# Two matmuls with a GELU between: b's first load ahead of a's, two banks for the first transposes, a's first cast on two engines

## The chip, the core and the metric

The kernel runs on one core of a Trainium2 chip. The metric is the device time of one execution in microseconds (us), taken as the median of several executions.

## The reference

```python
def reference(a, b, c):                 # a 1024x1024, b 1024x2048, c 2048x1024, all float32
    h = np.matmul(a, b)
    h = 0.5 * h * (1 + np.tanh(np.sqrt(2 / np.pi) * (h + 0.044715 * h ** 3)))
    return np.matmul(h, c).astype(np.float32)
```

So two products with a tanh-approximated GELU between them.

## The kernel before

The matmuls run in bf16 (and, in the later stages, on fp32 sums made from bf16 pieces); everything accumulates in fp32 in PSUM, whose eight banks are named by number (`bank(i)`). The order of work on every engine is the order in which the Python code issues it: the kernel uses a manual schedule, and only waits are derived from the tiles. An instruction therefore stands in the queue of its engine behind everything written above it for that engine.

The work has three stages. The first (lines 214 to 294) computes the first 512 columns of h, transposed, in eight blocks of 128 x 512: `ps[h, t]` is tile t (0 to 3) of h's columns for row half h (0 or 1) of a. The second stage (`seven(zero, ...)` and `seven(one, ...)`) makes the other 1536 columns of h, the third (`seven(two, ...)`) the product with c; both use seven products of half-size blocks in place of eight, with sums and differences made on VectorE (DVE). The change touches the first stage only.

**Loads.** The first stage starts with nothing in SBUF. SyncE (SP) issues twelve loads of 512 KB each (lines 76 to 82): `load_a(h, q)` brings 256 columns (q of 4) of row half h of a, `load_b(q)` brings two 128-row tiles of b's first 512 columns. They arrive as fp32 in the staging tiles `sta` and `stb`. All loads of b's other columns and of c are issued by GpSimd (POOL) behind a copy (`gate`, line 84) that waits for a late load of a.

**From a load to a product.** A piece of b needs one cast to bf16: `cast_b(k)` (line 136) is one ScalarE (ACT) instruction into `b1`, or, with n=2, two on half the columns each. A piece of a needs more, since TensorE wants it transposed: `cast_a(h, q, *engs)` casts 128 x 1024 elements into a bf16 tile `ab`, on one engine or in two halves on the engines named (line 99 is ACT, line 101 DVE). `turn(h, q, i, ab)` is a generator: at each `next` it issues four TensorE transposes into one half of the PSUM tile `pt` (line 132) and one DVE copy of that half to `aT` (line 133). Its two steps bring the k tiles 2q and 2q+1. In the kernel before both steps write halves of the same bank.

**Products.** `block(h, tiles, ks)` issues for each k in ks and each t in tiles one matmul of 128 x 128 weights (from `b1`) by 128 x 512 (from `aT`), all on line 105. `stir(*widths)` (line 116) issues matmuls of a zeroed fp32 tile whose result nobody reads, to keep TensorE busy while it would wait; one call shows as two records for each width.

**The order around the change** (before, lines 214 to 238): four fillers of width 256; the cast of a's piece (0, 0) on DVE alone; its transposes in bank 4 with fillers between; b's tiles 0 and 1; the cast of a's piece (1, 0) on DVE and ACT; six products of row half 0; the transposes of (1, 0), in bank 7, around two more products; then the first products of row half 1 (line 234) into banks 4, 5 and 6. From there on, loads, casts, transposes and products alternate in the same way (lines 239 to 294).

Of the kernel before, what the change touches and what calls it, by code (L numbers as in the profile page):

```python
# [11 lines left out]
BF16 = mybir.dt.bfloat16  # L12
# [7 lines left out]
def kernel(ctx, tc, a, b, c, out):  # L20
    nc = tc.nc
    M, K = a.shape
    _, N = b.shape
    _, P = c.shape
    H = 512
# [17 lines left out]
    def bank(i, shape=(128, H), dt=F32, name="ps"):  # L43
        return pp.tile(list(shape), dt, name=name, tag=f"bank{i}", padded_shape=None)

    def pieces(tag, bufs, shape, dt, name):
        return small.tile(shape, dt, name=name, tag=tag, bufs=bufs)
# [21 lines left out]
    def load_a(h, q):  # L69
        nc.sync.dma_start(out=sta[q // 2][:, h, q % 2],  # L70
                          in_=av[:, 4 * h:4 * h + 4, ds(q * 256, 256)])

    def load_b(q):
        nc.sync.dma_start(out=stb[:, 2 * q:2 * q + 2], in_=bv[:, 2 * q:2 * q + 2, 0:H])

    load_a(0, 0)
    load_b(0)
    load_a(1, 0)
    for q in range(1, 4):
        load_a(0, q)  # L80
# [16 lines left out]
    def copy(eng, dst, src):  # L97
        if eng is nc.scalar:
            nc.scalar.activation(dst, src, AF.Copy)  # L99
        else:  # L100
            nc.vector.tensor_copy(dst, src)  # L101
# [11 lines left out]
    def stir(*widths):  # L113

        for w in widths:
            nc.tensor.matmul(ps[0, 3][:, 0:w], warm[:, 0:128], warm[:, 0:w],  # L116
                             start=True, stop=True, skip_group_check=True)

    def cast_a(h, q, *engs):

        ab = pieces("ab", 2, [128, 4, 256], BF16, "ab")
        for i, eng in enumerate(engs):
            w = 256 // len(engs)
            copy(eng, ab[:, :, ts(i, w)], sta[q // 2][:, h, q % 2][:, :, ts(i, w)])
        return ab

    def turn(h, q, i, ab):

        pt = bank(i, (128, 2, H), BF16, "pt")
        for n in range(2):  # L130
            for m in range(4):
                nc.tensor.transpose(pt[:, n, ts(m, 128)], ab[:, m, ts(n, 128)], ident)  # L132
            nc.vector.tensor_copy(aT[:, h, 2 * q + n], pt[:, n])  # L133
            yield

    def cast_b(k, n=1):
        for i in range(n):
            r = ds(i * (H // n), H // n)
            nc.scalar.activation(b1[:, k, r], stb[:, k, r], AF.Copy)  # L139

    def block(h, tiles, ks):
        for k in ks:
            for t in tiles:
                mm1(ps[h, t], t, h, (k,))
# [66 lines left out]
    zero = Seven(4, quarters(b1, H, 256), BB, [None] * 4, [None] * 4, 2)  # L211
    one = Seven(4, quarters(b2, 0, H), BB, [None] * 4, zero.t)

    stir(256, 256, 256, 256)
    tn = turn(0, 0, 4, cast_a(0, 0, nc.vector))
    next(tn)
    stir(256)
    next(tn)
    stir(128)
    cast_b(0, 2)  # L220
    cast_b(1)
    ab = cast_a(1, 0, nc.vector, nc.scalar)
    block(0, range(4), (0,))
    block(0, range(2), (1,))
    tn = turn(1, 0, 7, ab)
    next(tn)
    block(0, range(2, 4), (1,))
    next(tn)
    for t in range(3):
        ps[1, t] = bank(4 + t)  # L230
    zero.t[0], zero.t[1] = pair(2)
# [1 line left out]
    ab = cast_a(0, 1, nc.scalar, nc.scalar)  # L233
    block(1, range(3), (0,))
    tn = turn(0, 1, 7, ab)
    next(tn)
    block(1, range(3), (1,))
# [3 lines left out]
    ab = cast_a(1, 1, nc.vector, nc.scalar)  # L241
    block(0, range(4), (2,))
    block(0, range(1), (3,))
    tn = turn(1, 1, 7, ab)
# [4 lines left out]
    ab = cast_a(0, 2, nc.scalar, nc.scalar)  # L249
    block(1, range(3), (2,))  # L250
    tn = turn(0, 2, 7, ab)
# [5 lines left out]
    ab = cast_a(1, 2, nc.vector, nc.scalar)  # L257
    block(0, range(4), (4,))
    block(0, range(1), (5,))
    tn = turn(1, 2, 7, ab)  # L260
# [4 lines left out]
    ab = cast_a(0, 3, nc.scalar, nc.scalar)  # L265
    block(1, range(3), (4,))
    tn = turn(0, 3, 7, ab)
# [6 lines left out]
    ab = cast_a(1, 3, nc.scalar, nc.vector)  # L274
# [6 lines left out]
    tn = turn(1, 3, 0, ab)  # L281
# [213 lines left out]
```

## Time and profile before

| what | value |
|---|---|
| time, median of 3 | 118.26 us (117.88 to 118.27) |
| span of the profiled execution | 116.2 us |
| TensorE busy | 111.7 us (96%), 540 matmul records |
| VectorE busy | 90.3 us (78%) |
| ScalarE busy | 59.3 us (51%) |
| twelve first loads | 512 KB each; 3.5 us from issue to landing for the first, 8.4 us in the median for a's |

A line of the profile names an engine, the line of the code, the operation, and the tiles written and read (`pt<-ident,ab`). PE is TensorE's matmul side, PEld its weight loads, SPq and POOLq the queues from which loads are issued. In the timeline the first two numbers are start and duration in us from the start of the span; in brackets stands how long the engine was idle before, and what ended that. The chain of work follows the end of the kernel back through what released each step; in order of time it gives start, duration and what ran.

### The profile page before, as it was taken

The page shows a single profiled execution, that of the slowest core. Times are in us where ns is not written, and L with a number is a line of the kernel's source. Part 1 is how long each engine was busy: PE and PEld are TensorE (multiplying, and loading weights), DVE is VectorE, ACT ScalarE, POOL GpSimd, SP SyncE. Part 2 cuts the span into 40 slices and gives each one's busy share as a digit, 9 for nine tenths or more (in the row PEclk, how much of TensorE's full clock was granted, in tenths as well). Part 3 has the DMA queues.
Part 4 walks back from the last instruction along what each step waited for, and adds up shares of the span by engine and source line. Part 5 has one row for each costly group of instructions (what it writes and reads, how often), then busy time and mean ns, then how long its engine had stood idle before and what let it go on. Part 6 is the DMA issues. An engine that isn't in the chain of part 4 may idle for free.

```text
span 116.2 us, 1478 instructions
## 1 busy us (share of the span) xinstructions
PE 111.7 (96%) x540; PEld 76.9 (66%) x540; DVE 90.3 (78%) x107; ACT 59.3 (51%) x99; POOL 11.0 (9%) x21
## 2 busy tenths in 40 slices
PE   5999999999999999999999999999999999999980
PEld 4655555545777447888885444588888888888860
DVE  0336666889998999844699999999999986954770
ACT  5067668989269998066699329600034982000000
POOL 2000049623322000000000000000000000000000
PEclk9999999999999999999999999999999999999999
DMA  2999999999999999998000000070000002014993
GB/s 83 298 356 393 395 395 321 206 206 206 206 208 213 211 213 211 213 209 164 4 0 0 0 6 0 7 264 0 0 0 0 0 0 96 0 69 171 370 364 109
DMA packets 13542, 17.91 MB, mean 154 GB/s; under 512 B 736, under 2 KB 8928, under 8 KB 13536
## 3 DMA queue, kind: packets, MB, share of 16 engines
q0 software_dynamic: 5344, 7.34, 35.6%
q1 hardware_dynamic: 8192, 10.49, 25.2%
q8 instruction: 4, 0.07, 0.2%
q14 instruction: 2, 0.02, 0.0%
HBM read 20.97 MB, written 4.19 MB: 217 GB/s over the span
## 4 chain that ended last, share of the span: by engine, by line
PE 96%; DVE 1%; issue 0%
PE ps L197 76%; PE ps L105 12%; PE ps L116 4%; PE pt L132 4%; DVE aT L133 0%; DVE ot L382 0%; DVE warm L50 0%
## 5 line engine op out<-in xcount | busy, mean ns | idle before, releaser
L197 PE MATMUL ps<-x,s 128*128 128x512 f32 x128 | 29.6, 391 | 0.0
L197 PEld LDWEIGHTS ps<-x,s 128*128 128x128 f32 x128 | 24.0, 188 | 5.1
L197 PE MATMUL ps<-x,x 128*128 128x512 f32 x96 | 22.9, 394 | 0.0
L197 PEld LDWEIGHTS ps<-x,x 128*128 128x128 f32 x96 | 18.0, 188 | 3.9
L105 PE MATMUL ps<-aT,b 128*128 128x512 bf16 x64 | 16.3, 379 | 0.0
L305 ACT ACTIVATE v<-ps 128x512 f32<-128x512 f32 x10 | 6.0, 598 | 19.4 <-PE ps L197 19.4
L197 PE MATMUL ps<-c_sb,hT 128*128 128x512 bf16 (+1 forms) x72 | 14.2, 356 | 0.0
L197 PE MATMUL ps<-x 128*128 128x512 f32 x56 | 13.2, 393 | 0.0
L197 PEld LDWEIGHTS ps<-x 128*128 128x128 f32 x56 | 10.2, 188 | 2.7 <-ACT u L305 0.4
L133 DVE COPY aT<-pt 128x512 bf16<-128x512 bf16 x16 | 6.8, 424 | 6.4 <-PE pt L132 6.4
L197 PEld LDWEIGHTS <-hT 128*128 128x128 bf16 x72 | 6.9, 98 | 7.0 <-issue 0.5
L109 ACT ACTIVATE hT<-ot 128x512 bf16<-128x512 f32 x18 | 10.5, 625 | 1.5 <-DVE ot L310 1.3
L310 DVE TENSOR_TENSOR ot<-ps,v 128x512 f32<-128x512 f32 x10 | 6.7, 688 | 5.2 <-DMA out_dram<-ot 3.8
L197 PE MATMUL ps<-aT,b 128*128 128x512 bf16 x48 | 10.7, 379 | 0.0
L310 DVE TENSOR_TENSOR ot<-ps,u 128x512 f32<-128x512 f32 x10 | 6.7, 689 | 5.1 <-ACT u L305 5.1
L155 DVE TENSOR_TENSOR x<-c_sb 128x1024 fp32r<-128x1024 bf16 x8 | 9.2, 1221 | 0.0
L132 PEld LDWEIGHTS <-ab 128*128 128x128 bf16 x64 | 4.9, 102 | 5.5 <-DVE ab L101 1.9
L197 PEld LDWEIGHTS <-b 128*128 128x128 bf16 x48 | 4.6, 97 | 5.7 <-issue 0.3
L105 PEld LDWEIGHTS <-b 128*128 128x128 bf16 x64 | 5.5, 98 | 4.1 <-ACT b L139 0.5
L99 ACT ACTIVATE ab<-sta 128x512 bf16<-128x512 f32 x10 | 6.0, 625 | 3.3 <-DMA sta<-in_a_dram 3.3
L305 ACT ACTIVATE u<-ps 128x512 f32<-128x512 f32 x10 | 5.8, 596 | 3.4 <-PE ps L197 3.2
L109 ACT ACTIVATE hT<-ps 128x512 bf16<-128x512 f32 x14 | 7.3, 596 | 0.4 <-PE ps L105 0.3
(39 smaller groups left out, 115.6 us busy)
## 6 DMA issues: line engine op xcount, KB each, us to landing
sta<-in_a_dram SPq DMA_DIRECT2D x8, 512.0 KB, 8.4
c_sb<-in_c_dram POOLq DMA_DIRECT2D x8, 512.0 KB, 19.9
b<-in_b_dram POOLq DMA_DIRECT2D x6, 512.0 KB, 11.5
out_dram<-ot SPq DMA_DIRECT2D x12, 256.0 KB, 2.1
stb<-in_b_dram SPq DMA_DIRECT2D x4, 512.0 KB, 8.0
out_dram<-ot SPq DMA_DIRECT2D x8, 128.0 KB, 2.0
```

The lines of the kernel that those rows point to most:

```text
L99: nc.scalar.activation(dst, src, AF.Copy)
L105: nc.tensor.matmul(p, b1[:, k, ts(t, 128)], aT[:, h, k], start=(k == 0), stop=(k == KT - 1))
L109: nc.scalar.activation(hT[h][:, t], p, AF.Gelu_apprx_tanh)
L116: nc.tensor.matmul(ps[0, 3][:, 0:w], warm[:, 0:128], warm[:, 0:w], start=True, stop=True, skip_group_check=True)
L132: nc.tensor.transpose(pt[:, n, ts(m, 128)], ab[:, m, ts(n, 128)], ident)
L133: nc.vector.tensor_copy(aT[:, h, 2 * q + n], pt[:, n])
L155: nc.vector.tensor_tensor(out=dst[:, r], in0=x[:, r], in1=y[:, r], op=op)
L197: nc.tensor.matmul(p[:, ds(c0, w)], l[:, k, ts(j, 128)], r[:, k, ds(c0, w)], start=(start and k == 0), stop=(k == self.kt - 1), skip_group ...
L305: nc.scalar.activation(st, p, AF.Copy)
L310: nc.vector.tensor_tensor(out=ot, in0=p, in1=st, op=ADD)
```

## The change

b's first load is issued ahead of a's first load. b's two first tiles are cast before a's first piece, each in one instruction. a's first piece is cast in halves on DVE and ACT. `turn` may be given two banks, one for each step, and the first two turns (a's pieces (0, 0) and (1, 0)) use this, so that the second four transposes can be written while the first are being copied. The fillers are arranged anew: six of width 256 ahead of everything, and one of width 64 after each step of the first turn. The transposes of (1, 0) now go all ahead of the two last products of tile k = 1. The aim is an earlier start of the real products.

```diff
+    load_b(0)
     load_a(0, 0)
-    load_b(0)
     load_a(1, 0)
     for q in range(1, 4):
         load_a(0, q)
@@ turn
-        pt = bank(i, (128, 2, H), BF16, "pt")
+        banks = i if isinstance(i, tuple) else (i,)
+        pts = [bank(x, (128, 2, H), BF16, "pt") for x in banks]
         for n in range(2):
+            pt = pts[n % len(pts)]
             for m in range(4):
                 nc.tensor.transpose(pt[:, n, ts(m, 128)], ab[:, m, ts(n, 128)], ident)
             nc.vector.tensor_copy(aT[:, h, 2 * q + n], pt[:, n])
@@ order of the first stage
-    stir(256, 256, 256, 256)
-    tn = turn(0, 0, 4, cast_a(0, 0, nc.vector))
-    next(tn)
-    stir(256)
-    next(tn)
-    stir(128)
-    cast_b(0, 2)
+    stir(256, 256, 256, 256, 256, 256)
+    cast_b(0)
     cast_b(1)
+    for _ in turn(0, 0, (4, 5), cast_a(0, 0, nc.vector, nc.scalar)):
+        stir(64)
     ab = cast_a(1, 0, nc.vector, nc.scalar)
     block(0, range(4), (0,))
     block(0, range(2), (1,))
-    tn = turn(1, 0, 7, ab)
-    next(tn)
+    for _ in turn(1, 0, (7, 6), ab):
+        pass
     block(0, range(2, 4), (1,))
-    next(tn)
```

## The prediction

> **What bounds the kernel now.** I read the chain of work first, to learn which engine carries the end. On the page:
>
> ```profile
> ## 4 chain that ended last, share of the span: by engine, by line
> PE 96%; DVE 1%; issue 0%
> PE ps L197 76%; PE ps L105 12%; PE ps L116 4%; PE pt L132 4%; DVE aT L133 0%; DVE ot L382 0%; DVE warm L50 0%
> ```
>
> TensorE carries the whole span, so a microsecond is won or lost only where TensorE does something other than real work. Line 116 (the filler `stir`) is such a place. The chain in order of time says where the real work starts:
>
> ```profile
> 1.19 3.78 PE ps L116 x8
> 4.97 0.01 issue
> 4.99 0.61 PE pt L132 x4
> 5.59 0.96 PE ps L116 x2
> 6.55 0.35 PE pt L132 x4
> 6.90 0.28 PE ps L116 x2
> 7.18 1.32 PE ps L105 x6
> 8.50 0.35 PE pt L132 x4
> 8.85 0.02 issue
> 8.88 0.44 DVE aT L133
> 9.31 0.04 issue
> 9.36 0.38 PE pt L132 x4
> 9.74 0.65 PE ps L105 x3
> ```
>
> Until about 7 us TensorE only fills and transposes; after 9.36 the chain never leaves it until 113. So the end moves by just as much as the first product of row half 1 (line 234), which starts at 9.57 in the timeline. Between 7.03 and 9.57 lies one real hole: DVE's copy at 8.88, for which the second set of transposes waits because both sets share bank 7.
>
> What the start waits for, from the timeline of ACT and DVE:
>
> ```profile
> 6.56 1.24 ACT L139 ACTIVATE b<-stb 128x256 bf16<-128x256 f32 x3 [4.33 <-DMA stb<-in_b_dram]
> 4.24 0.69 DVE L101 CAST ab<-sta 128x1024 bf16<-128x1024 f32 x1 [3.10 <-DMA sta<-in_a_dram]
> 7.96 0.43 DVE L101 CAST ab<-sta 128x512 bf16<-128x512 f32 x1 [0.59 <-DMA sta<-in_a_dram]
> 8.88 0.43 DVE L133 COPY aT<-pt 128x512 bf16<-128x512 bf16 x1 [0.49 <-PE pt L132]
> ```
>
> The first load (a) is in SBUF at 4.2, the second (b) at 6.5, the third (a, other half) at 7.95. The answers on the tiles give the shortest times from issue to landing, 3.5 for `sta` and 5.3 for `stb`; with the issues at 0.74 and 1.23 that is the same 4.2 and 6.5.
>
> **What the Trainium skill says.** TensorE: Matmul & The Clock Gate, Part 1 (the HAM clock gate): TensorE starts at half clock and gets the full one after a busy window of about 3.4 us that doesn't begin with the kernel. The trace agrees: four transposes take 0.61 at 4.99 but 0.40 at 8.44, and the fillers' spacing (starts at 3.48 and 3.91) is 0.43 a pass, while from 7.03 three products take 0.65. The clock rose between about 6 and 7. PSUM — Partial Sum Buffer, section on PSUM bank collisions: reading and writing one bank must be kept apart by a semaphore. The trace agrees: copy ends 9.31, transposes go at 9.36. DMA: Bandwidth & Descriptors, Queues, rings and completion order: loads of one issuing engine use the same rings in order, and one counts as landed only when its slowest share is down. The landings in order of issue agree.
>
> **The change part by part.** *Loads swapped.* No bytes change. b's first load now takes first place and lands about 4.3 by the 3.5 us of a first load. a's first lands second; call that L. Upper bound: the pair has the same bytes, so 6.54, where the pair is complete today. Lower bound: 4.2 plus 0.52 MB at the 394 GB/s seen from 3 to 4 us (1.33), so 5.5. Between them stands a question: from 4 to 6 us only 223 and 268 GB/s flow, while b's rows come in. If b's rows are what is slow, the swap merely moves the slow stretch; some of it then overlaps the slow beginning (258 GB/s from 2 to 3). I take L = 6.3.
>
> *b's casts first, in two whole instructions.* 2 x 0.61 on ACT from 4.3 to 5.5, before a is there: hidden by the wait for a. This removes today's limit at 7.03 (two half casts at 0.40 and a whole one, for which weight loads waited 0.5 in all).
>
> *a's first piece cast on two engines.* DVE's half takes 0.43, as at 7.96, instead of 0.69; ACT's 0.63 beside it. The first transposes need only DVE's half. ACT's half is done at L+0.66, but the first four transposes are issued until about L+0.73 and a 64-wide filler follows, so it costs nothing. Gain on this stretch 0.26.
>
> *Two banks.* The second transposes no longer wait for the first copy. For row half 1 this takes out the hole (8.91 to 9.36), but not all of it counts: line 234's product also needs its copy.
>
> *Fillers.* Six 256-wide ones, 12 passes of 0.43 = 5.12, from 1.19 to 6.31; they run while nothing else can, if L is 6.3. The 64-wide ones run while DVE copies.
>
> Now the path. From L to the first real product: start of cast 0.03, DVE half 0.43, to the transposes 0.05, transposes to copy 0.44 (8.44 to 8.88), copy 0.43, to TensorE 0.05: 1.43. Today only one half cast (0.42) and 0.05 stand behind the second landing, so the swap puts the long chain behind the late load and the short one behind the early load. With L = 6.3 the first product is at F = 7.73 instead of 7.03. From F on, TensorE needs six products (6 x 0.216 = 1.30), eight transposes (2 x 0.22) and two products (0.43): 2.17. The copy allows line 234 at F + 1.30 + 0.44 + 0.43 + 0.05 = F + 2.22, the later of the two. Its third product writes bank 6, free after the second copy: 0.43 later, just when two products are through; cost nothing. So line 234 starts at 9.95 instead of 9.57: **+0.38 us**. The third load at 7.95 doesn't matter then: its casts (DVE about 8.2 to 8.6, ACT 8.0 to 8.6) are done before F + 1.30 = 9.03.
>
> Behind the delayed casts DVE has its copies and `t1` (0.68), which fit the same spacing as now (t1 done at F+3.3, the next copy due at F+3.3). Nothing later absorbs a delay, for TensorE is dense to the end. Nothing adds to it either: later loads are in time by more than they are now.
>
> **The rivals.** *No change.* The swap repairs the slow stretch and L is 5.5 to 5.9. Then fillers set the start: they leave TensorE at 6.31, the transposes to copy take 0.64 at half clock (4.99 to 5.63), copy 0.43, 0.07 of handing over: F = 7.45, line 234 at 9.67, +0.10. For it: the slow stretch is no property of b's loads in general, since 374 to 400 GB/s flow later with b's loads among them. Against: it appears exactly in place two. About 118.35.
>
> *Faster.* The clock rises earlier, as it may if the window isn't tied to the kernel, the fillers shrink, and the loads come sooner: L = 5.5 gives F = 6.93 and line 234 at 9.15, -0.42. Against it: the sixth load's transposes go at 12.51, where the chain has 12.65; unless the loads too come earlier, only 0.14 can be kept. Take -0.3, about 118.0.
>
> *Clearly slower.* TensorE is now idle from about 6.5 to 6.8 and for some 0.4 before F. If the clock needs an undisturbed window, its rise slips by up to one window, by the skill's 3.4 us, and products from 7.7 to about 10 run at half speed: about half of 2.3 us more, so +1.2 with +0.38: 119.8. For it: today's long row of fillers up to 7 had no hole. Against: the holes are short.
>
> **How the numbers follow.** Later product with L from 6.1 to 6.54 (+0.2 to +0.6): 0.50. No change: 0.22. Faster: 0.14. Clearly slower: 0.14. The likeliest gives 118.26 + 0.38 = 118.6. The range reaches down past the faster case (-0.45, 117.8) and up to the upper bound of L (+0.62) and part of the slipped clock: 119.2. Half a per cent is 0.59 us. Only the far end of the faster case passes that, with an unknown help from the loads: 0.11. Slower by over 0.59: the slipped clock and the top third of the likeliest case, 0.31. Within: 0.58.
>
> **What would show it.** Right: `stb` landed near 4.3 and `sta` between 6.1 and 6.5; ACT idle between b's casts and its half of a; first L105 product at 7.5 to 8.0; no DVE piece in the chain between the two sets of transposes of row half 1; the first L105 product after them 0.2 to 0.6 later than 9.57, and the product's chain equally dense from there. Wrong: `sta` landed well before 6, or the transposes starting as soon as the fillers end; and if transposes after 7 us still take 0.61 for four, the clock has slipped.

## The result, and the profile after

The changed kernel takes 119.07 us (median of four, 118.98 to 119.15) against 118.27 us before: ratio 1.0072, 95% interval 1.0045 to 1.0099. A second measurement of the same two kernels gives 119.11 against 118.19, ratio 1.0073 (1.0061 to 1.0085). So the change costs about 0.8 to 0.9 us. The forecast was 118.6 in a range of 117.8 to 119.2: the direction of its likeliest case holds, but its 0.38 us is less than half of the loss.

The timeline of the changed kernel at the start, first ACT and DVE, then TensorE (start, duration; in brackets idle time and what ended it):

```profile
5.39 1.15 ACT L141 ACTIVATE b<-stb 128x512 bf16<-128x512 f32 x2 [3.15 <-DMA stb<-in_b_dram]
6.86 0.43 DVE L101 CAST ab<-sta 128x512 bf16<-128x512 f32 x1 [5.72 <-DMA sta<-in_a_dram]
7.34 0.40 PE L134 MATMUL pt<-ident,ab 128*128 128x128 bf16 x4 [1.32 <-DVE ab L101]
8.26 1.46 PE L105 MATMUL ps<-aT,b 128*128 128x512 bf16 x6
9.55 0.61 PE L134 MATMUL pt<-ident,ab 128*128 128x128 bf16 x8
```

b is in at 5.4 and not at 4.3, a at 6.85 and not at 6.3. TensorE has run out of fillers and waits 1.3 us for the cast. The first product starts at 8.26 where it was 7.03. The same view a little later shows the first product of row half 1 (still called line 234 below), which was at 9.57:

```profile
10.45 0.81 PE L105 MATMUL ps<-aT,b 128*128 128x512 bf16 x3
```

That is 0.88 later. A second loss appears where the forecast expected nothing, around a's last load:

```profile
21.72 0.63 ACT L99 ACTIVATE ab<-sta 128x512 bf16<-128x512 f32 x1 [1.69 <-DMA sta<-in_a_dram]
22.89 0.38 PE L134 MATMUL pt<-ident,ab 128*128 128x128 bf16 x4 [0.28 <-ACT hT L109]
```

Before, the same two steps were

```profile
20.09 0.63 ACT L99 ACTIVATE ab<-sta 128x512 bf16<-128x512 f32 x1 [0.32 <-DMA sta<-in_a_dram]
21.70 0.39 PE L132 MATMUL pt<-ident,ab 128*128 128x128 bf16 x4
```

a's last load lands 1.6 us later than before, although the load ahead of it is only 0.3 late. ACT executes in order: its cast of that piece stands ahead of the four GELUs (line 109), and the last transposes need bank 0, which the first GELU releases. So one late load holds the GELU, and the GELU holds TensorE. That the two losses don't simply add is to be expected: TensorE, late by 0.8 already, comes to the second place when part of that wait is over.

The theory at this point: the swap makes the start late, all else of the change is harmless. The rival: the rearranged banks, casts and fillers cost something themselves.

### The profile page after: what moved, and what is told of

It is laid out like the page before. It is cut to its first block, busy times and chain, and to the rows that moved or that the text cites. A ratio compares the mean times of both kernels' runs of the same rounds, so it can differ in the third digit from the quotient of the medians.

```text
span 117.3 us, 1481 instructions
## 1 busy us (share of the span) xinstructions
PE 110.9 (95%) x538; PEld 77.4 (66%) x544; DVE 90.0 (77%) x107; ACT 59.7 (51%) x99; POOL 11.2 (10%) x21
## 3 DMA queue, kind: packets, MB, share of 16 engines
q0 software_dynamic: 5344, 7.34, 35.3%
## 4 chain that ended last, share of the span: by engine, by line
PE 78%; SPq 9%; DMA 8%; ACT 1%; issue 1%; DVE 0%; ACTq 0%
PE ps L199 75%; DMA sta<-in_a_dram 8%; SPq L70 6%; SPq L74 3%; PE ps L105 2%; ACT ab L99 1%; PE pt L134 1%; ACT hT L109 0%; DVE ot L380 0%; ACTq L99 0%; ACTq L189 0%
## 5 line engine op out<-in xcount | busy, mean ns | idle before, releaser
L105 PE MATMUL ps<-aT,b 128*128 128x512 bf16 x62 | 15.7, 379 | 0.1
L199 PE MATMUL ps<-aT,b 128*128 128x512 bf16 x46 | 10.6, 379 | 0.1
L99 ACT ACTIVATE ab<-sta 128x512 bf16<-128x512 f32 x11 | 6.6, 625 | 5.6 <-DMA sta<-in_a_dram 5.6
L134 PE MATMUL pt<-ident,ab 128*128 128x128 bf16 x64 | 6.0, 218 | 1.7 <-DVE ab L101 1.3
```

Of the source, the lines that this page charges most:

```text
L105: nc.tensor.matmul(p, b1[:, k, ts(t, 128)], aT[:, h, k], start=(k == 0), stop=(k == KT - 1))
L199: nc.tensor.matmul(p[:, ds(c0, w)], l[:, k, ts(j, 128)], r[:, k, ds(c0, w)], start=(start and k == 0), stop=(k == self.kt - 1), skip_group ...
```

## The experiments

### One part of the change at a time

**Only the loads swapped**, on the kernel before:

```diff
-    load_a(0, 0)
-    load_b(0)
+    load_b(0)
+    load_a(0, 0)
```

> The kernel before with b's first load ahead of a's first, and nothing else of the change. My theory: the order of the two loads is the loss, because it puts the long way (cast, transposes, copy) behind the later landing, which is at 6.8 us in the changed kernel. Here the way is longer than in the changed kernel (whole cast 0.69, one bank, so the second transposes wait for the first copy): first product at about 8.9, line 234 at about 11.4 against 9.57, so about 120.0, a ratio near 1.015. Rival (the rearranged fillers, banks and casts are the loss, the order of loads is not): no slower than 0.3% against before.

Measured: 121.72 against 118.21, ratio 1.0298 (1.0269 to 1.0326), twice the expected loss. The swap is bad, but its mechanism was only half of it. TensorE's timeline:

```profile
7.65 0.40 PE L132 MATMUL pt<-ident,ab 128*128 128x128 bf16 x4 [2.69 <-DVE ab L101]
8.57 0.58 PE L132 MATMUL pt<-ident,ab 128*128 128x128 bf16 x4
9.47 2.55 PE L105 MATMUL ps<-aT,b 128*128 128x512 bf16 x6
```

With four fillers TensorE stands idle for 2.69 us. Its six first products then take 2.55 and not 1.47. In the table of stretches, where the third figure from the right is the granted TensorE clock, one sees why:

```profile
7.00:8.00 1.00, 0.35 (x5) 0.35 (x6) 0.59 (x1) 0.00 (x0) 0.00 (x0) 1.00 1.08 383
8.00:9.00 1.00, 1.00 (x8) 0.67 (x7) 0.43 (x1) 0.63 (x1) 0.00 (x0) 0.63 1.10 403
9.00:10.00 1.00, 1.00 (x6) 0.66 (x5) 0.76 (x2) 0.24 (x1) 0.00 (x0) 0.50 1.05 394
10.00:11.00 1.00, 1.00 (x4) 0.36 (x3) 0.00 (x0) 0.95 (x3) 0.00 (x0) 0.50 1.08 386
11.00:12.00 1.00, 1.00 (x6) 0.42 (x5) 0.00 (x0) 1.00 (x2) 0.00 (x0) 0.67 1.09 385
```

The clock was up when TensorE began again (the four transposes at 7.65 take 0.40) and falls to half soon after, for over three microseconds. In the changed kernel, whose longer row of fillers leaves TensorE idle for only 1.3 us, four transposes take 0.40 at 7.34 and six products 1.46, the figures of the full clock. So the longer row belongs to the swap; its worth alone was not measured.

**All but the swap**: the changed kernel with a in front again.

```diff
-    load_b(0)
     load_a(0, 0)
+    load_b(0)
@@
-    cast_b(0)
-    cast_b(1)
     for _ in turn(0, 0, (4, 5), cast_a(0, 0, nc.vector, nc.scalar)):
         stir(64)
+    cast_b(0)
+    cast_b(1)
```

> The changed kernel with a's first load in front again (and, so that ScalarE does not wait for b with a's half cast behind it, that cast ahead of b's two). My theory: a lands near 4.2, b near 6.5, first product at about 7.25, line 234 at 9.45 instead of 9.57; then the transposes of a's sixth load, whose cast ends at 12.46, take back what was gained: 118.2, ratio 0.997 to 1.002. Rival (the rest of the change costs): ratio 1.004 or more.

Measured: 118.94, ratio 1.0061 (1.0049 to 1.0073). My theory falls: with the loads in the old order nearly the whole loss is still there. It isn't at the start, where the first product comes at 7.36 and line 234 at 9.57, as before. It is at a's last load, as in the changed kernel:

```profile
21.53 0.63 ACT L99 ACTIVATE ab<-sta 128x512 bf16<-128x512 f32 x1 [1.44 <-DMA sta<-in_a_dram]
22.70 0.38 PE L134 MATMUL pt<-ident,ab 128*128 128x128 bf16 x4 [0.49 <-ACT hT L109]
```

**Two banks alone**, on the kernel before:

```diff
-    tn = turn(0, 0, 4, cast_a(0, 0, nc.vector))
+    tn = turn(0, 0, (4, 5), cast_a(0, 0, nc.vector))
-    tn = turn(1, 0, 7, ab)
+    tn = turn(1, 0, (7, 6), ab)
```

> The kernel before with two banks for the first two turns and nothing else. My theory: the second transposes of row half 1 go at 9.11 instead of 9.36 and line 234 at 9.36 instead of 9.57, but the transposes at 12.51 wait for a cast of a landed load, as they do now within 0.02, so the end does not move: ratio 0.998 to 1.001. Rival (TensorE alone sets the end, so a hole that is closed is won): -0.2 us, ratio 0.998 or less.

Measured: 118.23 against 118.21, ratio 1.0002 (0.9994 to 1.0010), a last load not late, and no gain. The weight loads show what takes the closed hole back:

```profile
10.36 0.23 PEld L134 LDWEIGHTS <-ab 128*128 128x128 bf16 x4 [0.57 <-ACT ab L99]
12.75 0.23 PEld L134 LDWEIGHTS <-ab 128*128 128x128 bf16 x4 [0.43 <-DVE ab L101]
```

Line 234 starts 0.1 sooner, at 9.47, and the next transposes then wait for casts. The second of these casts, whose other half is ACT's, waits for its load (ACT starts at 12.27 after 0.25 us, and the bracket names the load); in this execution the load is also 0.2 us later than in the profiled one of before. That nothing is won is shown by the medians. In this stage TensorE and the loads are nearly even: a hole closed ahead of a piece that arrives when it arrives is worth nothing.

### Why a's last load is late

Both late kernels have eight fillers where the kernel before has six. The page counts four packets of instruction fetches (queue q8, 0.07 MB together). One filler shows as two matmul records, each with its weight load, so two fillers more are eight instructions. If a fetch is due when so many TensorE instructions are used up, they bring it forward against the program; that was the theory. The DMA answers for three short stretches of the changed kernel fit it: the queue lines of 19.6 to 19.9, of 20.2 to 20.5 and of 20.5 to 20.8 us are

```profile
q0 software_dynamic: 50, 0.05, 103.9%
q8 instruction: 1, 0.02, 20.0%
q1 hardware_dynamic: 14, 0.01, 11.9%
...
q0 software_dynamic: 56, 0.06, 116.7%
...
q0 software_dynamic: 60, 0.06, 124.4%
q1 hardware_dynamic: 2, 0.00, 3.1%
```

q1 carries the loads issued by SP. The fetch begins in the first stretch, at 19.61, and its one packet takes 0.96 us. In the second stretch no packet of a's load moves at all, and two stragglers follow in the third. Meanwhile GpSimd's loads (q0) take the engines. That is a coincidence in time and no proof, so three runs change only the number of fillers.

**The kernel before with two short fillers more:**

```diff
-    stir(256, 256, 256, 256)
+    stir(256, 256, 256, 256, 64, 64)
```

> The kernel before with two 64-wide fillers more in its first row of fillers, as many TensorE instructions in the first stage as the changed kernel has. New theory: the instruction fetch, one 16 KB packet of about 0.96 us on one DMA engine near 19.5, comes at a place set by how many TensorE instructions have been used up; two more bring it forward by about 0.3 us against the program, into the tail of a's last load, whose remaining packets on that engine then wait, so that this load lands near 21.5 and not near 20.1. Expected: last sta landing 21.3 to 21.7, ratio 1.004 to 1.007. Rival, the late landing comes from the new arrangement of banks, casts and transposes: landing near 20.1, ratio 0.999 to 1.001.

Measured: 118.88 against 118.21, ratio 1.0054 (1.0042 to 1.0066). Nothing else was touched, and line 234 starts at 9.55 as before. ACT and TensorE at the last piece:

```profile
21.31 0.63 ACT L99 ACTIVATE ab<-sta 128x512 bf16<-128x512 f32 x1 [1.49 <-PE ps L105]
22.47 0.38 PE L132 MATMUL pt<-ident,ab 128*128 128x128 bf16 x4 [0.54 <-ACT hT L109]
```

The bracket names TensorE, whose product had long been done; DVE's cast of the other half starts at 21.32 too and names the load. Two fillers whose result nobody reads cost 0.6 to 0.7 us some 16 us later. Where they stand they cost nothing: they put the first transposes at 5.51 instead of 4.99, but the first product waits for b anyway (7.00 and 7.03).

**All but the swap, with two fewer** (the two 64-wide ones left out):

```diff
     for _ in turn(0, 0, (4, 5), cast_a(0, 0, nc.vector, nc.scalar)):
-        stir(64)
+        pass
```

> The kernel of the run all_but_swap without the two 64-wide fillers, so with as many TensorE instructions as before. New theory (instruction fetch): a's last load lands near 20.2 again and the ratio falls from 1.006 to 0.998 to 1.001. Rival (the arrangement itself): landing near 21.4, ratio 1.005 or more.

Measured: 118.23 against 118.21, ratio 0.9999 (0.9988 to 1.0011). The cast of the last piece starts after a wait of 0.29 instead of 1.44:

```profile
20.72 0.63 ACT L99 ACTIVATE ab<-sta 128x512 bf16<-128x512 f32 x1 [0.29 <-DMA sta<-in_a_dram]
```

**The changed kernel with two fewer**, the same edit:

> The changed kernel without its two 64-wide fillers. They hide behind VectorE's copies, so the first product stays near 8.25. New theory: a's last load lands near 20.2 and what remains of the loss is the later start, about 0.88 at line 234 less what the waits for casts near 12.5 and 16.5 had left idle: ratio 1.003 to 1.006, under the changed kernel's 1.007. Rival, the start alone is the whole loss: 1.007 as for the changed kernel.

Measured: 118.77 against 118.21, ratio 1.0051 (1.0038 to 1.0064). The last load is in time and TensorE no longer waits for the GELU:

```profile
20.46 0.63 ACT L99 ACTIVATE ab<-sta 128x512 bf16<-128x512 f32 x1 [0.35 <-DMA sta<-in_a_dram]
22.53 0.39 PE L134 MATMUL pt<-ident,ab 128*128 128x128 bf16 x4
```

So the number of fillers is shown to be the cause, by adding two to one kernel and taking two from two others. It holds for every profile of this case: the five with eight fillers (two of them follow below) have the late load, the nine with six do not. GpSimd's loads are not the difference: they begin at 18.9 in the kernel before with and without the two fillers.

That the fetch is the link can be read from the packets and landings in the traces. A load is cut into sixteen shares, each with a landing of its own, and counts as landed with the last one:

| kernel | fillers | fetch from, to | packets of a's last load not begun when the fetch begins | fifteen shares in | all sixteen in |
|---|---|---|---|---|---|
| before | 6 | 19.30, 20.26 | 45 | 19.95 | 19.99 |
| before, two more | 8 | 19.09, 20.06 | 99 | 20.06 | 21.20 |
| all but the swap | 8 | 19.34, 20.30 | 44 | 20.33 | 21.43 |
| the same, two fewer | 6 | 19.40, 20.36 | 41 | 20.17 | 20.61 |
| changed | 8 | 19.61, 20.57 | 16 | 20.26 | 21.61 |
| changed, two fewer | 6 | 20.99, 21.97 | 0 | 20.25 | 20.35 |

In the late kernels one share alone is missing for over a microsecond. In all five late profiles no packet of this load begins for the last 0.36 to 0.74 us of the fetch, and the next one begins 0.01 us before the fetch ends. The trace doesn't name the DMA engine of a packet, but five such meetings leave little room for chance: the missing share stands behind the fetch. Part of the delay comes after that (in the changed kernel the last packet ends at 20.70, the landing comes at 21.61; before, 19.65 and 19.99), and isn't explained.

How the number of fillers decides this is open. In the kernel before two more do bring the fetch forward, as the theory had it. But that is not enough: all but the swap has its fetch at about the same time with eight fillers and with six, with as many packets to come, and only with eight does it harm; in the kernel before it does none either. So it may be the engine that the fetch falls on that differs. That wasn't separated.

The changed kernel once more, for a closer interval:

> The changed kernel itself, in a job of its own with the kernel before, to put a closer interval on its loss. Theory of two terms (late start 0.55, late last load 0.3): ratio 1.0065 to 1.008, last sta landing near 21.5. If the late last load is a chance of single executions: ratio near 1.005 and landing near 20.3.

Measured: 119.11 against 118.19, ratio 1.0073 (1.0061 to 1.0085), the last load late again. The changed kernel's loss thus has two terms: 0.56 us (118.77 - 118.21) for the late start, and for the late last load what is left of 0.80 to 0.92, so 0.24 to 0.36 us. These are differences of medians; the intervals of the two ratios leave the second term anywhere from about 0.05 to 0.5. It is smaller here than the 0.7 that it costs where the start is not late, for TensorE comes later to the place.

### Why b's first load is slow

The late start comes from a landing of 6.85. Its root is that b's first load flows slowly, in first place too. In the changed kernel (last two figures: DMA share, GB/s):

```profile
2.00:3.00 1.00, 1.00 (x3) 0.78 (x3) 0.00 (x0) 0.23 (x2) 0.00 (x0) 1.00 0.76 199
3.00:4.00 1.00, 1.00 (x4) 0.75 (x3) 0.00 (x0) 0.00 (x0) 0.00 (x0) 1.00 0.94 201
4.00:5.00 1.00, 1.00 (x4) 0.81 (x3) 0.00 (x0) 0.00 (x0) 0.00 (x0) 1.00 0.96 301
5.00:6.00 1.00, 1.00 (x4) 0.50 (x3) 0.00 (x0) 0.61 (x2) 0.00 (x0) 1.00 1.08 376
```

Before, a's load ran at 394 GB/s from 3 to 4, and 223 and 268 followed from 4 to 6, while b's came in. The slow stretch has moved with b.

**Other rows of b first.** The k pieces of the first stage go in the order 1, 0, 2, 3, on the changed kernel; the edit renames pieces throughout lines 76 to 281, its core is

```diff
-    load_b(0)
-    load_a(0, 0)
-    load_a(1, 0)
-    for q in range(1, 4):
+    load_b(1)
+    load_a(0, 1)
+    load_a(1, 1)
+    for q in (0, 2, 3):
```

> The changed kernel with the order of k pieces in the first stage 1, 0, 2, 3 instead of 0, 1, 2, 3: b's first load is then rows 256 to 511, a's columns follow, and every k pair is used in that order. It tells why b's first load flows slowly (landed 5.37, at 240 GB/s or less, in whichever place it stands). Theory A, whatever of b is read first is slow: stb lands near 5.4 and sta near 6.8 again, time within 0.3% of the changed kernel, ratio about 1.007. Theory B, it is those rows: stb lands near 4.3, sta near 5.7, first product near 7.2 and ratio near 1.000; the slow rows then show in the fifth load.

Measured: ratio 1.0056 (1.0042 to 1.0071). ACT casts b from 5.41 and a from 6.77, as in the changed kernel (5.39, 6.86). It isn't the rows. The interval includes the expected 1.007, and the last load is as late as there.

**A touch of b ahead** of all loads, on the kernel before:

```diff
+    nc.sync.dma_start(out=room, in_=bv[:, KT - 1, 0:16])
     load_a(0, 0)
     load_b(0)
```

> The kernel before with one small load of b (16 columns of its last 128 rows used here) issued ahead of everything. b's first load flows slowly in whichever place and with whichever rows. Theory A, the first access to b is what is slow: b's first load then moves at its later rate, 4.0 to 6.0 us show about 390 GB/s instead of 223 to 268, stb lands near 5.9 although everything is issued 0.45 later, and later loads are earlier by 0.3, ratio 0.997 to 1.000. Theory B, loads with 2 KB rows are slow early whatever was read: stb lands near 7.0 (6.55 and 0.45), ratio about 1.003.

Measured: ratio 1.0140 (1.0091 to 1.0189), slower than either theory had it. The executions fell into two groups, 119.0 to 119.1 and 120.5 to 120.9, so this ratio is a mixture; the profiled one is of the second group. For the loads it shows that a landed at 5.1, not at 4.65 (4.2 and the 0.45 of the issue), b at 6.8, and from 5 to 6 us 250 GB/s flowed. A slow stretch remains; a touch ahead is no cure.

The same trace shows two costs that have nothing to do with b. The fillers end at 4.97 as before, and the transposes start at 5.90 after a hole of 0.93:

```profile
8.22 2.59 PE L106 MATMUL ps<-aT,b 128*128 128x512 bf16 x6
10.65 0.39 PE L133 MATMUL pt<-ident,ab 128*128 128x128 bf16 x4
```

Six products take 2.59 instead of 1.47, and four transposes take 0.61 at 5.90 and 0.63 at 7.26: in this execution TensorE ran at half speed until after 10 us. The 1.1 us lost on the products is most of the 1.5 between the groups, so the faster one may be that in which the clock rose in time; no execution of it was profiled. The other cost stands at the very end. From the start of the kernel's last addition on DVE (115.39) to the end of the span (119.1) 3.7 us pass, where they are 3.2 before (113.00 and 116.2). In the trace SyncE closes with nine checks of its transfers. Before, eight of them are through when the last store lands and one follows; with one load more, one is through and eight follow, 0.06 us each. So an added load costs about 0.4 us here that a landing can't show.

**b's first load in two halves of 256 columns**, so in rows of 1 KB like a's, on the kernel before, alone and with two banks:

```diff
-    load_b(0)
+    for c in range(2):
+        nc.sync.dma_start(out=stb[:, 0:2, ts(c, 256)], in_=bv[:, 0:2, ts(c, 256)])
```

> The kernel before with b's first load issued as two loads of 256 columns each, so in 1 KB rows like a's. A touch of b ahead did not cure the slow flow of b's first load. Theory A, rows of 2 KB are what stalls early: the two loads flow at about 390 GB/s from 4 to 6 us, b is in by about 5.9 and later loads come 0.5 earlier; TensorE's own start then limits, ratio 0.996 to 0.999. Theory B, b's first load is slow whatever its rows: in by about 6.5, 220 to 270 GB/s from 4 to 6 us, ratio 0.999 to 1.002.

> The run b_halves and two banks for the first two turns together. If b_halves brings the loads earlier, the hole closed by the two banks (0.2 us at line 234) is no longer taken back by the wait for a's sixth load: ratio 0.994 to 0.997. If b_halves changes nothing, neither does this: 0.999 to 1.002.

Measured: ratios 1.0092 (1.0061 to 1.0124) and 1.0108 (1.0079 to 1.0137). Neither theory had a loss. 0.4 us of it is again the end behind the added load (3.7 us from the last addition on, in both kernels). Alone, the executions spread from 118.37 to 120.36, and the profiled one is the fastest, with its last product no later than before (112.60 and 112.70), so its trace doesn't show where the others lose. The profiled execution of the second kernel (118.87) has the load after b's at 8.4 and not at 7.9, and TensorE waits 0.72 us for its cast. Whether the others lose in that way stays open. For b's load the first trace is clear enough: it is in at 6.2 (6.5 before), and from 5 to 6 us 202 GB/s flow. Long rows are not the cause.

**b third**, behind two loads of a, on the kernel before, one execution:

```diff
     load_a(0, 0)
-    load_b(0)
     load_a(1, 0)
+    load_b(0)
```

> The kernel before with b's first load third, behind both first loads of a (issue order a, a, b). A look at the loads alone: is b's first load slow because it is early, or because it is b's first? Early: between 5.5 and 7.5 us, where b now flows, about 370 to 390 GB/s, and b lands about 1.4 behind the load ahead of it. b's first, whenever: 220 to 290 GB/s there, and b lands about 2.0 or more behind. The first product then waits for b (about 8.0 or 8.5), so the time is higher than before by 0.3 to 1.0 us and says nothing on the question.

```profile
4.00:5.00 1.00, 0.97 (x3) 0.25 (x1) 0.69 (x1) 0.00 (x0) 0.00 (x0) 1.00 1.11 384
5.00:6.00 1.00, 0.96 (x6) 0.88 (x7) 0.32 (x1) 0.00 (x0) 0.00 (x0) 1.00 0.99 255
6.00:7.00 1.00, 1.00 (x8) 0.72 (x6) 0.11 (x1) 0.00 (x0) 0.00 (x0) 1.00 0.87 203
7.00:8.00 1.00, 0.27 (x2) 0.07 (x1) 0.76 (x2) 0.00 (x0) 0.00 (x0) 1.00 0.94 283
```

Two loads of a run at full rate to 5 us, then b's first load pulls the rate down to 203. So it is slow in first, second and third place, with either set of rows, in long and in short ones. It isn't slow because it is early. What makes the first load of b slow, while the three later ones are not, these runs don't tell. The kernel's 121.40 is more than expected; the product at 9.2 comes after a hole of 2.0 us, and the half clock is back (mean granted clock 0.985).

No version tried beats the kernel before; the two-bank kernel and all_but_swap_two_fewer equal it.

## Why the prediction was right or wrong

**The bound.** TensorE's chain does carry the end, but it was not the only bound, as I had it: in the two-bank run a closed hole was taken back by casts of loads. "Nothing later absorbs a delay" is thus too strong. Line 234 is 0.88 late against the profiled execution of before, and 0.56 is left in the medians once the last load is in time; the traces separate the rest. In the changed kernel with two fillers fewer line 234 is 0.97 late, the last transposes of the stage 0.83 (22.53 and 21.70), and the whole execution 0.81 (118.81 and 118.00). So about 0.15 is absorbed on the way, and the other 0.2 is that the profiled execution of before was that much quicker than its median.

**The number.** 119.07 lies in the range, in part by luck: its upper end was set for a slipped clock, which didn't come. What filled it was a landing beyond my upper bound and a late last load that the sum didn't have. The loss of 0.7% is also more than the half per cent to which I had given 0.58.

**The landing L.** This is the step that failed first, as a size. I took 6.3, with 6.54 as an upper bound because "the pair has the same bytes". It was 6.85. That b's first load would keep its slow flow in first place was named as a possibility; that the slow beginning would hide part of it was wrong: from 2 to 4 us 200 GB/s flowed, less than a's 258 and 394 in the same place. The landing of 4.3 for b, taken from a's first load, was 5.4.

**The path behind it.** L + 1.43 gives 8.28 for the measured L; the first product started at 8.26. F + 2.22 gives 10.48; line 234 started at 10.45. The sums of half cast, transposes, copy and products were right, and so was the cost of nothing for ACT's half, the third product's bank and the third load.

**The banks.** The chain behind DVE's copy was taken out as said, and worth nothing, as the two-bank run shows for the kernel before.

**"Nothing adds to it either: later loads are in time by more than they are now."** This step failed outright. a's last load came 1.6 us later, and 0.24 to 0.36 us of the loss is that. I had costed two more fillers by the time that hides them. Their other cost, their number, was not in the sum. The profile of before did show the four fetches on its third part and when the last load landed, but nothing that ties them.

**The clock.** The clearly-slower case (a hole lets the clock rise late) did not come true for the changed kernel. The last of its filler records start 0.22 us apart and not 0.43, so the clock was up before the hole of 1.3 us, and stayed up. It did come true in the profiled execution with a touch of b ahead, after a hole of 0.93 us: 1.1 us lost on six products, near the forecast's 1.2. In the run with only the swap the clock had risen and fell again behind a hole of 2.69, a case that the prediction didn't have.

**The rivals with L of 5.5 to 5.9** (no change, faster) fell with L: a slow flow that moves with b can't be repaired by its place.

## What to carry to other kernels

Where two loads feed one start, put first the one with the longer way to the first product behind it: here 1.43 us stand behind a and 0.5 behind b, and the swap made the long way follow the late landing. Filler instructions are not free because nobody waits for them: they are instructions, and their number can decide whether a fetch holds up a load that is just in time, far from the edit. So when a small edit costs time at a place that it didn't touch, change the count of instructions alone, as two fillers did here, before blaming the edit's intent. And a variant with one more load can lose at the very end, so its total alone doesn't judge its start.

## What had not been expected of the hardware

Two 64-wide fillers ahead of the first transposes cost 0.6 us on the kernel before (ratio 1.0054), through a load that landed over a microsecond late some 16 us later. In each late profile fifteen sixteenths of that load were down in time and one share stood behind a single 16 KB instruction fetch of 0.96 us. An idle TensorE of 2.69 us was enough for half clock from about 8.3 to 11.7 us, and one of 2.0 us in the run with b third; 1.3 us at full clock did no harm in the changed kernel, while 0.93 us before the clock had risen went with half speed until after 10 us in the touch of b. One load of twelve, b's first, ran at about 180 to 280 GB/s in its slow microseconds whatever its place, rows or row length, where the others ran at 350 to 410. One more load by SyncE at the start added 0.4 us behind the last addition, in all three kernels that had one.
